# Spreading a norm over five units, ordering weight splits behind norm factors, and giving an operand rows of 512 floats

## The chip, the cores and the metric

The kernel runs on one core of a Trainium2 chip. The metric is device microseconds of an execution; the median of three executions of the kernel before is 1996.99 us (1993.12 to 1997.41). One further execution was profiled. PE is TensorE (matmul), PEld its weight loads, DVE is VectorE, ACT ScalarE, POOL GpSimd, SP SyncE; PE's clock is granted at one of two levels, 1.2 or 2.4 GHz.

## What is computed

Two transformer programs run one after the other on 256 tokens of width 1024. The first block has two layers: a mixer, a cross-attention to a memory of 256 tokens, and a SwiGLU (`silu(h @ w_gate) * (h @ w_up)) @ w_down`, hidden width 2816). The second block takes the first one's output as latents `h` and a second stream, Context `hc` (256 tokens), through two layers with adaptive modulation. Cut to what matters:

```
for l in range(2):
    mod, mod_c = silu(c) @ w_mod[l] + b_mod[l], silu(c_ctx) @ w_mod[l] + b_mod[l]
    ac = rms_norm(hc, norm1_g[l]) * (1 + csc1) + csh1      # Context's first norm
    a  = rms_norm(h,  norm1_g[l]) * (1 + sc1)  + sh1
    ... a @ w_in[l]: pooling, spatial gate, attention over h and Context's keys, gates
    h = h + g1 * mix
    h = h + g2 * square(relu(modulated_norm(h) @ w_ff1[l])) @ w_ff2[l]
    # Context has the same steps in layer 0; in layer 1 only its keys and values are used
return rms_norm(h, final_g)
```

All results are fp32. The kernel keeps that accuracy by splitting each operand into a high and a low part of a faster type (`hi`, and `lo = x - hi`) and by three matmuls for one.

## The kernel before, in words

**Splits.** Weights come in pieces of 128 x 1024 floats (512 KB) from memory, on SP's DMA queue. `pieces` (L210) loads one into a `raw` buffer (three of them) and splits it: ACT copies `hi` (L280), DVE subtracts `lo` (L281). There are four `hi` and four `lo` buffers, so that splits run up to four pieces ahead of PE. A block is one accumulation of PE: `s_block` (L230) has the weights stationary and streams the activation, `m_block` (L259) the other way round, each with three matmuls for every 128 rows (L226 to L228). `s_pair` (L240) streams `hi` and `lo` of the activation together as 512 columns (L247) and then `hi` with the weight's low part (L248); `pair_sum` (L252) adds the halves on ACT and DVE.

**Order.** The program's text is traced in order, and a planner orders each engine's queue from it: among what is ready the earlier traced goes first, with times that the planner works out beforehand. What is traced late can so be issued early, when nothing earlier is ready. An engine executes its queue strictly in that order. `tc.issue_after(x)` orders what is traced inside it behind `x` on `x`'s engine, without a wait for `x` to finish. PSUM has eight banks: three `mm`, two `sc`, two `pv`, one `fmm`.

**Operands.** `op` (L514) holds the current normalised activation, `hi` and `lo`, as `[128, 8 feature blocks, 2, 514]`: columns 0 to 255 are the latents, 256 to 511 Context, and the last two are used in layer 1 alone, when columns 256 to 513 hold the latents before normalisation (`raw`, L1186) with the two columns of the modulation's shift. Layer 1's first two feed-forward parts work on `raw` and scale the result by the row of norm factors afterwards (L1265), so that PE need not wait for the norm.

**A norm** is: squares on ACT (L318) summed on DVE (L335), token sums on PE (`token_sums`, L347, matmuls L354), an rsqrt chain of ten short DVE instructions (L363, L290 to L298), two transposes on PE that spread the factors over partitions (L371), an ACT copy of them (`rows`, L375), and for each of eight feature blocks a product on DVE (L921), the high part on ACT (L923) and the low part on DVE (L924) (`modulated`, L917).

**Where the norms stand.** Context's first norm is a hook in the second SwiGLU: `swiglu` (L792) runs eleven units, each `hidden` (gate and up blocks, an activation) and `down` (w_down blocks into four kept banks), and calls the hook `context` (L932) once, at unit 4: it finishes the modulation of layer 0 (`modulation_done`, whose weights come on POOL's DMA queue), loads Context, squares and sums it and normalises all eight feature blocks. In `layer` (L985) with two streams (layer 0) the order is: Context's block 2 of the first projection, `norm()` (final norm of the first block and layer 0's first norm in one, L1323), Context's block 3, `finish()` (latents' operand), the latents' blocks 0 and 1. Layer 0's feed-forward norm (L1217) comes after the `w_o` blocks of each stream in turn; its first four `w_ff1` pieces are traced after both (L1241). Layer 1's first norm of the latents (L1318) is traced between the last `w_ff2` blocks of the latents and those of Context; its first projection's pieces after all (L1003), and Context's norm (L1321) after the latents' two blocks.

**Branches.** `attnT`, `poolT` and `sguT` (L979 to L981) hold the three branches' results as separate `hi` and `lo` tiles; their last readers are the gate blocks, ahead of the `w_o` blocks at which `raw` is written.

The call of the hook and the operand, as they stand:

```
        for u in range(9):
            if hook is not None and u == 4:
                hook()
            down([hidden(u)], False)
        down([hidden(9), hidden(10)], True)
...
    op_all = pool.tile([128, KD, 2, 514], F32R, name="op")
    op = tuple(op_all[:, :, i, :] for i in range(2))
```

Of the kernel before, what the change touches and what calls it, by code (L numbers as in the profile page):

```python
# [106 lines left out]
def kernel(ctx: ExitStack, tc: tile.TileContext, A: dict, out: bass.AP):  # L107
# [101 lines left out]

    def pieces(name, group, then=None):  # L210

        res = []
        for off, k0, kt, n in OFFSETS[name][group]:
# [6 lines left out]
            split(hi, lo, raw)  # L220
# [38 lines left out]
    def m_block(ps, ws, act, t, k0=0, whole=None):  # L259
# [4 lines left out]
        for w in ws:  # L264
            for k in range(w.kt):
                a = w.k0 + k + k0
                mm3(ps, ah[:, a, sl], al[:, a, sl], w.hi[:, k, :], w.lo[:, k, :],
                    w is whole[0] and k == 0, w is whole[-1] and k == w.kt - 1)
# [78 lines left out]
    def token_sums(sums, tag="mm", ticks=3):  # L347
# [8 lines left out]
        tick(ticks, last)  # L356
        return ps
# [9 lines left out]
    def rows(cols, scales=(1.0,), tag="mm"):  # L367
# [146 lines left out]
    op_all = pool.tile([128, KD, 2, 514], F32R, name="op")  # L514
# [15 lines left out]
    mem = {}  # L530
# [261 lines left out]
    def swiglu(l, nrm, nxt, hook=None):  # L792
# [40 lines left out]
        for u in range(9):  # L833
            if hook is not None and u == 4:
                hook()
# [81 lines left out]
    def modulated(l, which, fb, s, g, row):  # L917

        a = s1("a")
        sh = modT[:, l, 24 * which + fb, s:s + 1]  # L920
        nc.vector.scalar_tensor_tensor(a, (xT, mem["n"])[s][:, fb, :], g[:, fb, s:s + 1], row, op0=OP.mult, op1=OP.mult)  # L921
        hi, lo = (x[:, fb, s * 256:s * 256 + 256] for x in op)
        nc.scalar.activation(hi, a, AF.Identity, bias=sh, scale=1.0)  # L923
        nc.vector.scalar_tensor_tensor(lo, a, sh, f(hi), op0=OP.add, op1=OP.subtract)  # L924

    def all_modulated(l, which, stream, acc, tag="mm"):
        (row,) = rows(rstd_cols([acc], tag), tag=tag)
        g = gains(l, which)
        for fb in range(KD):
            modulated(l, which, fb, stream, g, row)  # L930
# [48 lines left out]
    attnT = (pool.tile([128, 4, 512], F32R, name="ath"), pool.tile([128, 4, 512], F32R, name="atl"))  # L979
    poolT = (pool.tile([128, 2, 512], F32R, name="plh"), pool.tile([128, 2, 512], F32R, name="pll"))  # L980
# [504 lines left out]
```

## Time and profile before

| | |
|---|---|
| median of three executions | 1996.99 us (1993.12 to 1997.41) |
| the profiled execution, its own time | 1994.0 us |
| its span, first to last instruction | 1991.9 us |
| mean granted clock of PE | 0.991 |
| instructions | 32614, of them 12676 matmuls |

The span is what the trace's rows are measured in; 2.1 us of the execution lie around it. Busy time is time in which an engine has at least one instruction under way. PE's matmuls are pipelined and their ends are modelled, so a busy PE can still start matmuls at different spacings. A granted clock of 0.90 for a stretch means that a fifth of it ran at the lower level. Idle time is put down to what ended it.

### The profile page before, as it was taken

The numbers are of one execution on the slowest core, as the hardware profiler recorded it, in microseconds if no ns is written. First come the engines' busy times: TensorE is split into PE (matmuls) and PEld (weight loads), VectorE is DVE, ScalarE is ACT, GpSimd is POOL, SyncE is SP. The second block draws the span as 40 slices with busy tenths as digits, with TensorE's granted clock in tenths as the row PEclk, the third lists the DMA queues.
The fourth block names the chain that finished last, engine by engine and source line by source line (L and its number), as shares of the span: only waits on it lengthen the run. The fifth ranks groups of instructions, "written<-read, shape, count | busy, mean of one in ns | idle before, by whom it ended". The sixth has DMA issues, their size and how long they took to land.

```text
span 1991.9 us, 32614 instructions
## 1 busy us (share of the span) xinstructions
PE 1940.7 (97%) x12676; PEld 1701.0 (85%) x12676; DVE 1412.0 (71%) x2964; ACT 902.6 (45%) x1595; POOL 84.6 (4%) x163
## 2 busy tenths in 40 slices
PE   7999999999999899999999999999999999999998
PEld 6689999998988799698778888888888898899987
DVE  7677777777676777645677757777765855678897
ACT  5555555554554455424432234322223534555554
POOL 1100000000000000000011100110000000000000
PEclk9999999999999999999999999999999999999999
DMA  7746555553356555222245533444432422454553
GB/s 262 264 174 215 190 189 183 179 180 127 128 189 218 181 182 174 94 85 75 65 153 185 164 111 100 148 143 149 138 122 85 159 102 90 161 186 169 185 190 117
DMA packets 89771, 309.33 MB, mean 155 GB/s; under 512 B 10528, under 2 KB 15552, under 8 KB 89360
## 3 DMA queue, kind: packets, MB, share of 16 engines
q1 hardware_dynamic: 74048, 254.43, 37.3%
q0 software_dynamic: 15280, 52.28, 7.9%
q8 instruction: 100, 1.64, 0.3%
q14 instruction: 55, 0.45, 0.1%
q10 hardware_dynamic: 288, 0.52, 0.1%
HBM read 306.15 MB, written 1.05 MB: 154 GB/s over the span
## 4 chain that ended last, share of the span: by engine, by line
PE 92%; DVE 3%; issue 2%; ACT 1%; DMA 1%; POOL 0%; DVEq 0%; SPq 0%; POOLq 0%; ACTq 0%
PE mm L227 15%; PE mm L226 15%; PE mm L228 15%; PE mm L247 10%; PE mm L248 5%; PE sc L226 4%; PE sc L227 4%; PE sc L228 4%; PE pv L226 3%; PE pv L227 3%; PE pv L228 3%; PE sc L426 2%; PE pv L462 2%; PE pv L445 2%; DVE lo L281 1%
## 5 line engine op out<-in xcount | busy, mean ns | idle before, releaser
L280 ACT ACTIVATE hi<-raw 128x1024 fp32r<-128x1024 f32 (+2 forms) x466 | 489.6, 1054 | 714.8 <-PE mm L227 236.3
L281 DVE TENSOR_TENSOR lo<-raw,hi 128x1024 fp32r<-128x1024 f32 (+2 forms) x466 | 566.4, 1218 | 290.7 <-ACT hi L280 287.9
L226 PE MATMUL mm<-op,hi 128*128 128x256 f32 (+2 forms) x944 | 315.1, 336 | 3.9 <-ACT op L923 1.3
L227 PE MATMUL mm<-op,hi 128*128 128x256 f32 (+2 forms) x944 | 318.2, 338 | 0.0
L228 PE MATMUL mm<-op,lo 128*128 128x256 f32 (+2 forms) x944 | 318.0, 338 | 0.0
L247 PE MATMUL mm<-op,hi 128*128 128x512 f32 x872 | 310.8, 396 | 3.9 <-DVE g L256 3.6
L248 PE MATMUL mm<-op,lo 128*128 128x256 f32 x872 | 245.3, 281 | 0.0
L226 PE MATMUL mm<-hi,op 128*128 128x256 f32 (+2 forms) x704 | 210.3, 300 | 13.0 <-ACT hi L280 9.1
L227 PE MATMUL mm<-lo,op 128*128 128x256 f32 (+2 forms) x704 | 211.7, 301 | 1.3 <-DVE lo L281 1.3
L228 PE MATMUL mm<-hi,op 128*128 128x256 f32 (+2 forms) x704 | 209.7, 299 | 1.2 <-DVE op L284 1.2
L226 PEld LDWEIGHTS mm<-op,hi 128*128 128x128 f32 x944 | 178.7, 190 | 27.2 <-issue 3.4
L247 PEld LDWEIGHTS mm<-op,hi 128*128 128x128 f32 x872 | 165.3, 190 | 39.8 <-issue 4.3
L228 PEld LDWEIGHTS mm<-op,lo 128*128 128x128 f32 x944 | 178.8, 189 | 22.8 <-issue 2.9
L227 PEld LDWEIGHTS mm<-op,hi 128*128 128x128 f32 x944 | 178.9, 189 | 20.4 <-issue 1.4
L248 PEld LDWEIGHTS mm<-op,lo 128*128 128x128 f32 x872 | 165.1, 189 | 0.7 <-DVE gate L1172 0.4
L226 PEld LDWEIGHTS mm<-hi,op 128*128 128x128 f32 x704 | 136.0, 194 | 17.7 <-ACT hi L280 9.1
L227 PEld LDWEIGHTS mm<-lo,op 128*128 128x128 f32 x704 | 136.0, 193 | 9.8 <-issue 3.8
L228 PEld LDWEIGHTS mm<-hi,op 128*128 128x128 f32 x704 | 136.0, 193 | 8.3 <-issue 2.3
L161 POOL DMA_DIRECT2D mraw<-in_w_mod x96 | 51.5, 537 | 585.8 <-DVE modraw L163 579.6
L1192 DVE SCALAR_TENSOR_TENSOR xT<-pv,modT,xT 128x256 f32<-128x256 f32 x84 | 40.2, 481 | 43.1 <-PE pv L228 40.8
L163 DVE CUSTOM_DVE_ANT_0 fmm<-mraw,silu 128x512 f32<-128x512 f32 x96 | 66.7, 694 | 2.3 <-DMA mraw<-in_w_mod 2.3
L227 PE MATMUL sc<-hid,hi 128*128 128x512 f32 (+1 forms) x192 | 66.4, 346 | 1.6 <-DVE hid L1233 1.6
(349 smaller groups left out, 3822.8 us busy)
## 6 DMA issues: line engine op xcount, KB each, us to landing
raw<-in_w_ff SPq DMA_DIRECT2D x128, 512.0 KB, 3.3
raw<-in_w_in SPq DMA_DIRECT2D x84, 512.0 KB, 3.3
fraw<-in_w_mod POOLq DMA_DIRECT2D x48, 512.0 KB, 5.5
mraw<-in_w_mod POOLq DMA_DIRECT2D x96, 256.0 KB, 3.0
raw<-in_l_w_gate SPq DMA_DIRECT2D x44, 512.0 KB, 3.3
raw<-in_l_w_up SPq DMA_DIRECT2D x44, 512.0 KB, 3.3
raw<-in_l_w_down SPq DMA_DIRECT2D x44, 512.0 KB, 3.2
raw<-in_l_w_qkv SPq DMA_DIRECT2D x24, 512.0 KB, 3.5
```

Of the source, the lines that this page charges most:

```text
L161: nc.gpsimd.dma_start(out=w, in_=A["w_mod1"][c, i])
L163: nc.vector.tensor_tensor_reduce(out=w if s else bank("fmm"), in0=w, in1=silu[s][:, i * 512:i * 512 + 512], scale=1.0, scalar=0.0, op0=OP. ...
L226: nc.tensor.matmul(ps, ah, bh, start=start, stop=False, skip_group_check=shared)
L227: nc.tensor.matmul(ps, ah, bl, start=False, stop=False, skip_group_check=shared)
L228: return nc.tensor.matmul(ps, al, bh, start=False, stop=stop, skip_group_check=shared)
L247: nc.tensor.matmul(ps, w.hi[:, k, c0:c0 + 128], both[:, a], start=w is ws[0] and k == 0, stop=False)
L248: i = nc.tensor.matmul(ps[:, :256], w.lo[:, k, c0:c0 + 128], hi[:, a, :], start=False, stop=w is ws[-1] and k == w.kt - 1)
L280: nc.scalar.activation(hi, src, AF.Copy)
L281: nc.vector.tensor_sub(lo, src, f(hi))
L426: i = nc.tensor.matmul(ps, (ah, ah, al)[p], (bh, bl, bh)[p], start=p == 0, stop=p == 2)
L445: nc.tensor.transpose(ps[:, n:n + 128], P[t][:, c:c + 128], ident)
L1192: nc.vector.scalar_tensor_tensor(x, ps, gain, x, op0=OP.mult, op1=OP.add)
```

## The change

The hook is called at every unit: it loads Context and squares it at unit 3, finishes the modulation and works out the factors at unit 5 (in the `fmm` bank instead of an `mm` bank), and normalises three, three and two feature blocks at units 6, 7 and 8. In `modulated` each product on DVE is ordered behind the low part of the feature block two before. Splits of weights traced after a norm with `hold=True` are ordered on ACT behind the ACT copy of that norm's factors. Those norms are layer 0's first of the latents, layer 0's feed-forward norm of the latents, layer 1's first of the latents and layer 1's feed-forward norm. Pieces of the work that follows a norm are traced right after it, or before it in layer 1's feed-forward. At the start of layer 0, half of Context's block 3 is traced ahead of the norm and the other half ordered behind the norm's token sums; the latents' two blocks run piece by piece together (`early_blocks`, L617). In layer 1, Context's norm is ordered behind those blocks on PE. `op` has rows of 512 floats, the branches are one tile with `hi` and `lo` next to each other, and `raw` (now `unnormed`) lies in the same memory.

```diff
-    op_all = pool.tile([128, KD, 2, 514], F32R, name="op")
+    op_all = pool.tile([128, KD, 2, 512], F32R, name="op")
...
+    held = {}
     def pieces(name, group, then=None):
...
-            split(hi, lo, raw)
+            if "norm" in held:
+                with tc.issue_after(held["norm"].ins):
+                    split(hi, lo, raw)
+            else:
+                split(hi, lo, raw)
...
         tick(ticks, last)
+        held["sums"] = last
...
-            nc.scalar.activation(r, ps[:, :256], AF.Copy, scale=s)
+            i = nc.scalar.activation(r, ps[:, :256], AF.Copy, scale=s)
+            if hold:
+                held["norm"] = i
...
-                m_block(res[t][:, :n], [p], act, t, whole=w)
+                held["early"] = m_block(res[t][:, :n], [p], act, t, whole=w)
...
-            if hook is not None and u == 4:
-                hook()
+            if hook is not None:
+                hook(u)
...
+    def modulated(l, which, s, g, row, fbs=range(KD)):
+        lows = []
+        for fb in fbs:
...
+            if len(lows) > 1:
+                with tc.issue_after(lows[-2].ins):
+                    nc.vector.scalar_tensor_tensor(a, x, g[:, fb, s:s + 1], row, op0=OP.mult, op1=OP.mult)
...
+            lows.append(nc.vector.scalar_tensor_tensor(lo, a, sh, f(hi), op0=OP.add, op1=OP.subtract))
...
-    def context():
-        modulation_done(0)
-        mem["n"], acc = load_rows("ctx")
-        all_modulated(0, 0, 1, acc)
+    def context(u):
+        if u == 3:
+            mem["n"], mem["acc"] = load_rows("ctx")
+        elif u == 5:
+            modulation_done(0)
+            (mem["row"],) = rows(rstd_cols([mem["acc"]], "fmm"), tag="fmm")
+            mem["g"] = gains(0, 0)
+        elif u > 5:
+            modulated(0, 0, 1, mem["g"], mem["row"], range(3 * u - 18, min(3 * u - 15, KD)))
...
+    branches = pool.tile([128, 8 * 2 * 512], F32R, name="br")
+    parts = branches.rearrange("p (k a n) -> p a k n", k=8, a=2)
+    attnT, poolT, sguT = (tuple(parts[:, a, k:k + n, :] for a in range(2)) for k, n in ((0, 4), (4, 2), (6, 2)))
+    parts = branches[:, :KD * 2 * 272].rearrange("p (k a n) -> p k a n", k=KD, a=2)
+    unnormed = tuple(parts[:, a, :, 0:258] for a in range(2))
...
-            pooled_and_gated(2)
+            pg = pieces("w_in" + W, 6)
+            ps = mm()
+            m_block(ps, pg, op, 2)
+            pooled_and_gated(2, ps)
+            ps = mm()
+            m_block(ps, pg[:2], op, 3, whole=pg)
             finish, latents = norm()
-            pooled_and_gated(3)
+            with tc.issue_after(held["sums"].ins):
+                m_block(ps, pg[2:], op, 3, whole=pg)
+            pooled_and_gated(3, ps)
             finish()
...
+        for t, ps in enumerate(early_blocks(pg, op, 512)):
+            pooled_and_gated(t, ps)
+        if ns == 1:
+            with tc.issue_after(held["early"].ins):
+                norm()
...
-            raw = tuple(x[:, :, 256:514] for x in (op_all[:, :, 0, :], op_all[:, :, 1, :]))
+            raw = unnormed
...
-                all_modulated(l, 1, s, acc[s], "pv")
+                all_modulated(l, 1, s, acc[s], "pv", hold=s == 0)
+                if s == 0:
+                    first = [pieces("w_ff1" + W, j) for j in range(4)]
         else:
-            (row,) = rows(rstd_cols([acc[0]], "pv"), tag="pv")
+            first = [pieces("w_ff1" + W, j) for j in range(4)]
+            (row,) = rows(rstd_cols([acc[0]], "pv"), tag="pv", hold=True)
...
                 modulation_done(1)
-                all_modulated(l + 1, 0, 0, acc[0])
+                all_modulated(l + 1, 0, 0, acc[0], hold=True)
+                pg = pieces("w_in%d" % (l + 1), 6)
...
-            (row,) = rows(y[:, 2:4], tag="pv")
+            (row,) = rows(y[:, 2:4], tag="pv", hold=True)
```

## Rows read from the trace of the kernel before

**Rows 1.** The page, part 1: busy time, share of the span, instructions of each engine.

```profile
PE 1940.7 (97%) x12676; PEld 1701.0 (85%) x12676; DVE 1412.0 (71%) x2964; ACT 902.6 (45%) x1595; POOL 84.6 (4%) x163
```

**Rows 2.** Windows (us): length, busy time (instructions) by engine, granted clock, DMA share, GB/s.

```profile
655.00:690.00 35.00, 27.60 (x164) 25.08 (x163) 24.91 (x56) 16.26 (x29) 0.00 (x0) 0.90 0.43 143
...
700.00:760.00 60.00, 60.00 (x394) 54.84 (x393) 43.89 (x71) 30.44 (x50) 0.00 (x0) 1.00 0.54 184
...
793.50:833.00 39.50, 34.76 (x158) 25.60 (x157) 26.83 (x71) 19.05 (x38) 0.98 (x2) 0.91 0.32 107
...
1181.00:1206.00 25.00, 22.99 (x166) 22.59 (x166) 17.15 (x48) 9.78 (x18) 0.00 (x0) 0.86 0.25 85
...
1545.00:1575.00 30.00, 27.59 (x174) 23.77 (x172) 22.90 (x52) 16.13 (x28) 0.00 (x0) 0.94 0.44 158
...
1575.00:1600.00 25.00, 22.50 (x179) 21.59 (x176) 21.70 (x61) 10.04 (x20) 0.99 (x2) 0.93 0.44 148
...
1797.00:1829.00 32.00, 28.72 (x236) 28.16 (x235) 26.98 (x67) 18.70 (x34) 0.00 (x0) 1.00 0.46 161
```

**Rows 3.** Waits of PE: tile and line, releaser, us in total, times, longest.

```profile
PE sc L226 <- ACT qk L280: 5.1, 3, 3.8
...
PE mm L247 <- DVE g L256: 3.6, 1, 3.6
...
PE pv L354 <- DVE acc L335: 2.6, 2, 2.4
...
PE mm L226 <- DVE s L407: 2.4, 1, 2.4
```

**Rows 4.** Groups of DVE, 668 to 684: count, busy us, mean ns, idle before, releaser.

```profile
L281 DVE TENSOR_TENSOR lo<-raw,hi 128x1024 fp32r<-128x1024 f32 x5 | 6.1, 1224 | 4.6 <-ACT hi L280 4.6
...
L924 DVE SCALAR_TENSOR_TENSOR op<-a,modT,op 128x256 fp32r<-128x256 f32 x8 | 3.7, 480 | 0.0
...
L921 DVE SCALAR_TENSOR_TENSOR a<-memc,gain,rows 128x256 f32<-128x256 f32 x8 | 3.6, 479 | 0.0
```

**Rows 5.** Timeline, start of layer 0: start, us, instruction, idle before.

```profile
809.20 0.43 PE L371 MATMUL pv<-ident,sm 128*128 128x128 f32 x2 [2.63 <-DVE sm L298]
...
811.17 0.79 PE L226 MATMUL mm<-hi,op 128*128 128x512 f32 x1 [1.54 <-ACT op L923]
```

**Rows 6.** Windows of PE alone: `hid`, `op`; paired form on `hid`, on `op`.

```profile
1246.16:1267.92 21.76, 21.76 (x97) 1.00 0.45 147
...
1267.92:1290.30 22.38, 22.38 (x98) 1.00 0.43 142
...
1870.41:1874.57 4.16, 4.16 (x26) 1.00 0.49 182
...
720.53:726.13 5.60, 5.60 (x34) 1.00 0.48 164
```

**Rows 7.** Timeline of DVE and ACT, layer 0's feed-forward norm.

```profile
1184.81 0.16 DVE L363 TENSOR_SCALAR sm<-pv 128x2 f32<-128x2 f32 x1 [0.44 <-PE pv L354]
...
1188.40 1.23 DVE L281 TENSOR_TENSOR lo<-raw,hi 128x1024 fp32r<-128x1024 f32 x1
...
1189.55 0.15 DVE L298 SCALAR_TENSOR_TENSOR sm<-sm 128x2 f32<-128x2 f32 x1
...
1192.69 0.38 ACT L375 ACTIVATE rows<-pv 128x256 f32<-128x256 f32 x1 [1.13 <-PE pv L371]
```

**Rows 8.** Timeline of DVE and ACT, start of layer 1.

```profile
1554.35 0.15 DVE L298 SCALAR_TENSOR_TENSOR sm<-sm 128x2 f32<-128x2 f32 x1
...
1556.76 1.06 ACT L280 ACTIVATE hi<-raw 128x1024 fp32r<-128x1024 f32 x1 [1.14 <-PE pv L227]
...
1558.03 0.36 ACT L375 ACTIVATE rows<-mm 128x256 f32<-128x256 f32 x1
```

**Rows 9.** Groups of PE, shapes apart: paired form and one of three lines on `op`.

```profile
L247 PE MATMUL mm<-op,hi 128*128 128x512 f32 x872 | 310.8, 396 | 3.9 <-DVE g L256 3.6 <-ACT hi L280 0.3
...
L227 PE MATMUL mm<-op,hi 128*128 128x512 f32 x432 | 171.6, 397 | 0.0
```

More of the change, by code (lines that the diff above doesn't have):

```diff
@@ L266, in m_block @@
                 a = w.k0 + k + k0
-                mm3(ps, ah[:, a, sl], al[:, a, sl], w.hi[:, k, :], w.lo[:, k, :],
-                    w is whole[0] and k == 0, w is whole[-1] and k == w.kt - 1)
+                i = mm3(ps, ah[:, a, sl], al[:, a, sl], w.hi[:, k, :], w.lo[:, k, :],
+                        w is whole[0] and k == 0, w is whole[-1] and k == w.kt - 1)
+        return i
     def k_outer(jobs, act, n):
@@ L365, in rstd_cols, with rows @@
         return y
-    def rows(cols, scales=(1.0,), tag="mm"):
+    def rows(cols, scales=(1.0,), tag="mm", hold=False):
         ps = bank(tag)
@@ L915, in gains, with all_modulated @@
         return g
[L917 to L930, printed above, removed]
-    def context():
-        modulation_done(0)
-        mem["n"], acc = load_rows("ctx")
-        all_modulated(0, 0, 1, acc)
+    def modulated(l, which, s, g, row, fbs=range(KD)):
+        lows = []
+        for fb in fbs:
+            a = s1("a")
+            sh = modT[:, l, 24 * which + fb, s:s + 1]
+            x = (xT, mem["n"])[s][:, fb, :]
+            if len(lows) > 1:
+                with tc.issue_after(lows[-2].ins):
+                    nc.vector.scalar_tensor_tensor(a, x, g[:, fb, s:s + 1], row, op0=OP.mult, op1=OP.mult)
+            else:
+                nc.vector.scalar_tensor_tensor(a, x, g[:, fb, s:s + 1], row, op0=OP.mult, op1=OP.mult)
+            hi, lo = (x[:, fb, s * 256:s * 256 + 256] for x in op)
+            nc.scalar.activation(hi, a, AF.Identity, bias=sh, scale=1.0)
+            lows.append(nc.vector.scalar_tensor_tensor(lo, a, sh, f(hi), op0=OP.add, op1=OP.subtract))
+    def all_modulated(l, which, stream, acc, tag="mm", hold=False):
+        (row,) = rows(rstd_cols([acc], tag), tag=tag, hold=hold)
+        modulated(l, which, stream, gains(l, which), row)
+    def context(u):
[7 more added lines that the diff above has]
+            modulated(0, 0, 1, mem["g"], mem["row"], range(3 * u - 18, min(3 * u - 15, KD)))
     steps[0] = modulation_0()
@@ L1002, in layer, with pooled_and_gated @@
         mv = small.tile([128, 4, 2], F32, tag="mv", bufs=2, name="mv")
-        pg = pieces("w_in" + W, 6)
-        def pooled_and_gated(t):
-            ps = mm()
-            m_block(ps, pg, op, t)
+        def pooled_and_gated(t, ps):
             nc.scalar.activation(vt[:, t, :], ps[:, 256:], AF.Copy)
@@ L1240, in hidden @@
             if part == 0 and ns == 2:
-                ws = [pieces("w_ff1" + W, j) for j in range(4)]
                 for s in range(ns):
@@ L1244, in hidden @@
                         ps = mm()[:, :256]
-                        s_block(ps, ws[j], part_of(op, s))
+                        s_block(ps, first[j], part_of(op, s))
                         relu2(ps, hid, j, slice(s * 256, s * 256 + 256))
@@ L1252, in hidden @@
                     ps = mm() if j < 3 else bank("sc")
-                    w = pieces("w_ff1" + W, 4 * part + j)
+                    w = pieces("w_ff1" + W, 4 * part + j) if part else first[j]
                     if part == 0 and j < 3:
@@ L1300, in layer @@
             if part == 0 and ns == 1:
-                for fb in range(KD):
-                    modulated(l, 1, fb, 0, g2, row)
+                modulated(l, 1, 0, g2, row)
             second(part, *h)
@@ L1340, in finish @@
         def finish():
-            (row,) = rows(y[:, 2:4], tag="pv")
-            for fb in range(KD):
-                modulated(0, 0, fb, 0, gg, row)
+            (row,) = rows(y[:, 2:4], tag="pv", hold=True)
+            modulated(0, 0, 0, gg, row)
         def latents():
@@ L1350, in final_norm @@
         return finish, latents
-    context_norm = layer(0, 2, final_norm)
+    later = layer(0, 2, final_norm)
     fill.close()
-    acc = layer(1, 1, context_norm)
+    acc = layer(1, 1, later)
     ot = temp("memc", [128, 2, D])
```

12 lines of the change are left out of this document (3 added, 9 removed).

## The prediction, made before the changed kernel was run

> **What bounds the kernel now.** I began with the page's first part: PE is busy for 1940.7 of 1991.9 us, beside its weight loads no other engine over 71% [rows 1]. The reader should see that only 51 us of PE idleness exist, so the change can win from three things: idle stretches, matmuls that run on the lower clock after them, and the spacing of matmuls while PE is busy. I then cut the span into windows [rows 2]. The control stretch 700:760 has PE busy throughout at clock 1.00. The others hold the norms that the change touches; their idle time is the length less PE's busy time, and the granted clock tells what share ran at 1.2 instead of 2.4 GHz (0.90 is a fifth of the stretch at half speed, a tenth of its time lost):
>
> - 655:690, Context's norm in the swiglu: 7.4 idle, 3.5 lost to the clock
> - 793.5:833, start of layer 0: 4.7 and 3.5
> - 1181:1206, layer 0's feed-forward norm: 2.0 and 3.5
> - 1545:1575 and 1575:1600, start of layer 1: 2.4 and 1.8, 2.5 and 1.8
> - 1797:1829, layer 1's feed-forward: 3.3 and 0
>
> Together 36 us, the most that the ordering part can give. PE's waits [rows 3] say what ends the idleness: ACT and DVE, never a weight's landing directly. In each stretch the in-order queues of ACT and DVE hold weight splits beside the norm's short chain.
>
> **The change, step by step.** The profiled execution took 1994.0 us, 3.0 below the median 1996.99; I sum against 1994.0 and put 3.0 on at the end.
>
> **1. Context's norm spread over units.** Today hook 4 traces sixteen DVE instructions (eight L921, eight L924) of 0.48 us in one lump; between 668 and 684 they take 7.3 us of DVE beside five weight splits of 1.22 us, 6.1 [rows 4]. The pair sums and gating products that empty the `mm` banks come behind them, and PE waits 3.6 us for one of them (DVE g, L256) [rows 3]. After it, half of the window's clock loss follows, 1.7. Split into 3, 3 and 2 feature blocks, each later unit gets at most 6 x 0.48 = 2.9 us; in 700:760 DVE is idle for 60 - 43.9 = 16.1 us, over a quarter [rows 2], which hides that; the new order on DVE (each product behind the low part two blocks earlier) keeps them from bunching again. So 3.6 + 1.7 = 5.3 goes; I take 5.0. The window's other stall, PE waiting on ACT for `qk` (5.1 over three waits, the longest 3.8) [rows 3], is not in this lump. It belongs to splits held up while the last modulation weights and the next phase's loads go out, which the change re-traces but doesn't remove: 0. Bounds: 0 if the lump only moves, 7.4 + 3.5 = 10.9 if all goes. The ctx load (SP queue) and squares move from hook 4 to hook 3, 1 MB as before; no wait of PE names them [rows 3], so 0; the remaining modulation loads, on POOL, move from hook 4 to hook 5, and behind them on POOL stand only block 2's first loads, which need the modulation's memory. Moving sums and rows from `mm` to the `fmm` bank frees a bank that the swiglu uses; in the 5.0.
>
> **2. Start of layer 0.** After the token sums PE waits 2.63 for the rsqrt chain, turns the factors at 809.20, waits 1.54 for the first operand and starts at 811.17 [rows 5], then runs at the lower clock. The change leaves the second half of Context's block 3 for this hole: 2 pieces x 2 x 3 = 12 matmuls of 512 columns, at 22.38/96 = 0.233 us each [rows 6] 2.8 us. That covers the 2.63 wholly; the 1.54 stays. With idleness cut from 4.2 to about 1.6 I take the clock drop as avoided: 3.5 [rows 2]. `early_blocks` takes both token halves piece by piece, 6 matmuls or 1.4 us per feature block against 0.96 of DVE for its two instructions (2 x 0.48) [rows 4], so the operand is not late; but both halves then end together and their four ACT copies no longer hide behind the other half, about +1. 2.8 + 3.5 - 1 = 5.3; I take 5.0. Bounds: +1 (nothing covered, only the copies) to -8.2.
>
> **3. Layer 0's feed-forward norm.** The chain from L363 (1184.81) to L298 (1189.55) takes 4.7 us, with a 1.23 us split in it [rows 7]; at layer 0's start PE waits only 2.63 for a like chain [rows 5]. The factors are copied at 1192.69. Pinning the four splits behind that copy frees chain and copy, some 3 us; the price is that hi (1.06) [rows 8] and lo (1.23) [rows 7] of the first weight now come after it, on a DVE that has 16 x 0.48 to do as well. The pin is an order on ACT, no wait on another engine; behind a pinned split stand the norm's own ACT copies and stream 1's squares, each up to 1.06 later. Cover for this are stream 1's last `w_o` blocks on PE. I take 2.5 of the 5.5 there; bounds +3.7 (three splits of 1.23 that no longer lie ahead of the norm) and -5.5.
>
> **4. Start of layer 1.** The same shape: the chain ends at 1554.35, but a 1.06 split (1556.76) stands before the copy at 1558.03 [rows 8], and PE also waits 2.4 for stream 1's sums (DVE acc) [rows 3], which now queue behind the early blocks (behind them on PE only the factors' transposes; the keys of Context need those later). PE goes on instead with 48 matmuls of layer 1's first projection. Its four weight loads pass four small table loads on SP, nothing else. Nearly all of 2.4 + 1.8 should go: 4.0. The later stall (DVE s, 2.4 [rows 3]) comes from a DVE that stays as full: 0. Bounds +3.7 and -8.5.
>
> **5. Layer 1's feed-forward.** Hoisted first pieces and splits pinned behind the factors change the order on a DVE that is busy for 27.0 of 32 us [rows 2]; its sum is the same. 0; bounds +3.4 (a new clock drop like the others) and -3.3.
>
> **6. The operand without its two spare columns.** `op` shrinks from rows of 514 to 512 floats; the unnormalised operand goes to the branches' memory, whose readers finish before its first write, so no wait is added. What this may change is spacing. In 1267.92:1290.30 PE does four feed-forward blocks, 96 matmuls of 512 columns that stream `op`: 22.38 us, 233.1 ns each. Just before, the same form streams `hid` (rows of 512 floats): 96 in 21.76, 226.7 ns, both windows full and at clock 1.00 [rows 6] (the counts there include one or two still draining). The weights are laid out alike; the moving operand's place differs. Layer 0 has 3 x 432 such matmuls on `op` [rows 9]: 1296 x 6.4 ns = 8.4 us. The paired form costs 5.60/16 = 350 ns on `op` and 4.16/12 = 347 on `hid` [rows 6]: 872 pairs [rows 9] x 3 = 2.6. Of 11.0 I take 9.0, since each rate rests on one stretch. Bounds 0 to -11.
>
> Sentence apart: the Trainium skill (TensorE: Matmul & The Clock Gate, section Back-to-back issue gap) gives the spacing by the number of columns and the weight load, 518 cycles for 512 columns, with no term for where the operand lies; by it step 6 gives nothing and the sum is 16.5.
>
> **Sum:** 5.0 + 5.0 + 2.5 + 4.0 + 0 + 9.0 = 25.5. 1994.0 - 25.5 = 1968.5 for an execution like the profiled one, 1971.5 as a median; say **1971**.
>
> **Rivals.**
>
> *B, the spacing doesn't depend on the operand's place:* for it, that within a block the same operand is read by two neighbouring matmuls whose spacings differ; against it, that `hid` keeps one pace and `op` another in neighbouring windows. Then 1997 - 16.5 = 1980.
>
> *C, queue order doesn't follow trace order, or DVE's work decides:* the norms' instructions fill DVE wherever they go, and steps 1, 3 and 4 only move their stalls. For it, DVE's 27.0 of 32 and 21.7 of 25 us [rows 2]. Steps 2 and 6 stay: 1997 - 14 = 1983.
>
> *D, slower: the pinned split is the new last wait.* Place: the first matmul after each of the norms of steps 3, 4 and 5. Today three of four splits lie ahead of the norm; pinned, 3 x 1.23 = 3.7 us come behind the factors on DVE, and a longer hole adds a clock loss like the 3.5 seen: 7.1 at three sites, +21. It decides where PE reaches the first pinned weight before its lo is written. With steps 1 and 2 as above (-10) and B true: 2008. With step 6 working: 1999, no change that can be told.
>
> *E, the change does little at all* (the order comes out as before and the spacing too): 1997.
>
> **How the numbers follow.** A measurement of this kernel tells about 0.2%, 4 us, from no change. My forecast has 0.55, B 0.14, C 0.15, D with B 0.07, D with step 6 or E 0.09. Faster: 0.55 + 0.14 + 0.15 = 0.84; same 0.09; slower 0.07. The range: 1958 is the forecast with step 1's and step 4's whole ceilings (5.9 + 4.5 more, and 3 of step 3); 1990 takes in B and C with half of step 2 missing. The forecast alone would span 1960 to 1982.
>
> **What would show it.** Step 1: in the unit that now ends near 684, PE without the wait on DVE g and no clock drop after it. Step 2: PE's wait for L298 gone, clock 1.00 over the early blocks. Steps 3 and 4: no `hi` split between sums and factor copy, PE idle under 1 us. Step 6: `op` blocks at 21.8 us per 96. Wrong: first waits on `lo` after a norm (D), or `op` at 233 ns still (B).

## The result and the profile after

The changed kernel takes 1972.4 us (median of four executions, 1971.6 to 1974.46) against 1997.12 for the kernel before: ratio 0.9882, 95% interval 0.9865 to 0.99. The forecast was 1971. The profiled execution took 1973.03 us with a span of 1970.9. The total came out nearly as forecast; its terms did not. (For an execution like the profiled one the forecast was 1968.5, against 1973.03: the median fits better because the profiled execution of the kernel before lay 3 us below its median, and that of the changed kernel does not.)

The page's first part, as in [rows 1]:

```profile
PE 1929.8 (98%) x12676; PEld 1695.9 (86%) x12676; DVE 1411.6 (72%) x2964; ACT 902.6 (46%) x1595; POOL 84.8 (4%) x163
```

Of the 21.0 us by which the span shrank, 10.9 are PE time that was busy before (1940.7) and 10.1 idle time. The windows of [rows 2], moved so that each begins and ends with the same matmul by count (the length, then busy time of PE, PEld, DVE, ACT and POOL, then PE's clock):

```profile
656.36:681.16 24.80, 24.66 (x163) 22.46 (x162) 18.72 (x40) 12.84 (x21) 0.00 (x0) 1.00 0.62 207
691.08:751.45 60.37, 60.37 (x394) 54.95 (x393) 49.55 (x88) 33.73 (x58) 0.00 (x0) 1.00 0.53 184
785.17:818.85 33.68, 31.24 (x158) 23.68 (x156) 25.80 (x69) 18.08 (x37) 0.09 (x1) 0.95 0.36 125
1166.36:1188.40 22.04, 20.41 (x167) 19.81 (x166) 16.62 (x44) 9.70 (x17) 0.00 (x0) 1.00 0.29 96
1523.88:1552.43 28.55, 25.80 (x173) 22.80 (x172) 23.45 (x55) 15.73 (x27) 0.00 (x0) 1.00 0.38 133
1552.43:1575.32 22.89, 21.22 (x179) 20.17 (x176) 21.29 (x58) 10.34 (x19) 1.02 (x2) 1.00 0.43 151
1773.30:1806.07 32.77, 29.92 (x236) 28.93 (x235) 26.67 (x65) 18.18 (x33) 0.00 (x0) 0.97 0.44 156
```

Context's norm: 35 us became 24.80, both stalls and the low clock are gone. Layer 0's start: idle 4.7 became 2.4 (33.68 - 31.24), and the clock still falls (0.95). At layer 0's feed-forward norm and at layer 1's start PE is idle nearly as long as before (2.0 became 1.6; 2.4 + 2.5 became 2.75 + 1.67), but the clock stays at 1.00. Layer 1's feed-forward got longer. PE's waits, as in [rows 3] (the first is the start of the program):

```profile
PE mm L233 <- ACT hi L288: 9.0, 1, 9.0
PE mm L233 <- ACT op L941: 3.7, 3, 1.9
PE mm L254 <- ACT hi L288: 2.8, 2, 2.5
...
PE mm L234 <- DVE op L942: 1.1, 1, 1.1
PE mm L235 <- DVE op L942: 1.1, 1, 1.1
```

The waits for `qk` (3.8), `g` (3.6), the rsqrt chain (2.6) and `acc` (2.4) are gone; first operands and one weight of layer 1's feed-forward stand in their place.

**A table for all runs.** Every kernel issues 12,676 matmuls, so each trace gives the time at which PE begins the n-th. Below is the time that each stretch takes in each profiled execution, less that of the kernel before. The stretches begin in the kernel before at: start 0; A 164.8 (first block); B 636.7 (Context's norm); C 707.4 (to layer 0's start); D 844.5; E 1179.4 (layer 0's feed-forward norm); F 1221.6 (layer 0's feed-forward); G 1537.3 (layer 1's start); H 1598.8; I 1767.5 (layer 1's feed-forward, first parts); J 1878.1 to 1984.0.

```
kernel                start     A     B     C     D     E     F     G     H     I     J     A-J
the change              0.6   0.7 -10.1  -3.0  -2.8  -2.2  -4.3  -3.6   0.9   1.7   0.8  -21.9
E1 rows 512 alone      -0.6   0.6   0.9  -1.0  -2.8  -1.3  -4.3  -0.5   1.3   0.3   0.8   -6.0
E2 op 8 bytes on        3.5   2.6  -7.0  -1.6   0.4  -2.3   0.4  -1.9   0.9   2.3   0.8   -5.5
E11 rest 32 bytes on    6.1  -0.7 -10.2  -2.5  -0.0  -1.0   0.3  -1.9  -0.1   0.5   0.2  -15.5
E3 hook in mm           3.3   0.6  -8.3  -4.7  -2.8  -2.2  -4.3  -3.6   0.9   1.7   0.8  -21.9
E4 lump in fmm         -0.7   0.7  -8.0  -5.2  -2.8  -2.2  -4.3  -3.6   0.9   1.7   0.8  -22.1
E8 no half block        0.6   0.6 -10.2  -0.1  -2.8  -2.9  -4.3  -2.2   0.9   1.7   0.8  -18.4
E5 no pins              6.8   0.7 -10.5  -4.7  -2.8  -2.8  -4.3  -1.6   0.9   1.7   0.8  -22.5
E6 pin behind op       -0.3   0.7 -10.4  -3.0  -2.8  -2.6  -4.3  -2.4   0.9   1.6   0.8  -21.4
E7 no ff1 pin           2.0   2.1 -10.5  -4.6  -2.8  -2.2  -4.3  -3.6   0.9   1.7   0.8  -22.4
E9 no order             0.3   0.7  -9.9  -4.5  -2.8  -2.2  -4.3  -0.9   0.9   2.6   0.8  -19.6
E10 neither             1.2   0.7 -10.1  -3.0  -2.8  -1.3  -4.3   0.1   1.1   0.3   0.8  -18.5
E12 pin once            2.5   2.2 -10.2  -4.7  -2.8  -1.3  -4.3  -1.9   0.9   1.8   0.8  -19.5
```

Two things are to be seen. D, F and J repeat to 0.1 us in all kernels that share their code there. The start does not: it varies by 7 us between the profiled executions, though in all fourteen traces the instructions come in the same order up to A; E3 reaches A 2.7 us later than the changed kernel. There is one trace of each kernel, so whether one kernel's own executions differ as much there is not shown. I therefore don't rank kernels by medians that differ by less than about 5 us, but by the stretches, with the caution on the clock that comes below.

### The profile page after: what moved, and what is told of

Read it like the earlier page. It is cut to its first block, busy times and chain, and to the rows that moved or that the text cites. A ratio compares the mean times of both kernels' runs of the same rounds, so it can differ in the third digit from the quotient of the medians.

```text
span 1970.9 us, 32609 instructions
## 1 busy us (share of the span) xinstructions
PE 1929.8 (98%) x12676; PEld 1695.9 (86%) x12676; DVE 1411.6 (72%) x2964; ACT 902.6 (46%) x1595; POOL 84.8 (4%) x163
## 4 chain that ended last, share of the span: by engine, by line
PE 93%; DVE 3%; DMA 1%; issue 1%; ACT 1%; POOL 0%; DVEq 0%; SPq 0%; POOLq 0%; ACTq 0%
PE mm L233 15%; PE mm L234 15%; PE mm L235 15%; PE mm L254 10%; PE mm L255 5%; PE sc L233 4%; PE sc L234 4%; PE sc L235 4%; PE pv L233 3%; PE pv L234 3%; PE pv L235 3%; PE sc L437 2%; PE pv L473 2%; PE pv L456 2%; PE fmm L140 1%; DVE lo L289 1%
## 5 line engine op out<-in xcount | busy, mean ns | idle before, releaser
L234 PE MATMUL mm<-op,hi 128*128 128x256 f32 (+1 forms) x896 | 300.2, 336 | 1.1 <-DVE op L942 1.1
L235 PE MATMUL mm<-op,lo 128*128 128x256 f32 (+1 forms) x896 | 300.4, 337 | 0.0
L233 PE MATMUL mm<-op,hi 128*128 128x256 f32 (+1 forms) x896 | 297.9, 337 | 2.1 <-ACT relu L1261 1.1
L254 PEld LDWEIGHTS mm<-op,hi 128*128 128x128 f32 x872 | 163.9, 188 | 39.2 <-ACT hi L288 3.3
L235 PEld LDWEIGHTS mm<-op,lo 128*128 128x128 f32 x896 | 169.7, 189 | 21.2 <-issue 2.9
L233 PEld LDWEIGHTS mm<-op,hi 128*128 128x128 f32 x896 | 167.8, 189 | 22.7 <-issue 2.0
L234 PEld LDWEIGHTS mm<-op,hi 128*128 128x128 f32 x896 | 169.7, 189 | 20.1 <-issue 1.7
L255 PEld LDWEIGHTS mm<-op,lo 128*128 128x128 f32 x872 | 164.8, 189 | 1.0 <-DVE gate L1201 0.4
L163 DVE CUSTOM_DVE_ANT_0 mraw<-mraw,silu 128x512 f32<-128x512 f32 x96 | 66.1, 688 | 2.1
```

The costliest lines, as they stand in the source:

```text
L163: nc.vector.tensor_tensor_reduce(out=w if s else bank("fmm"), in0=w, in1=silu[s][:, i * 512:i * 512 + 512], scale=1.0, scalar=0.0, op0=OP. ...
L233: nc.tensor.matmul(ps, ah, bh, start=start, stop=False, skip_group_check=shared)
L234: nc.tensor.matmul(ps, ah, bl, start=False, stop=False, skip_group_check=shared)
L235: return nc.tensor.matmul(ps, al, bh, start=False, stop=stop, skip_group_check=shared)
L254: nc.tensor.matmul(ps, w.hi[:, k, c0:c0 + 128], both[:, a], start=w is ws[0] and k == 0, stop=False)
L255: i = nc.tensor.matmul(ps[:, :256], w.lo[:, k, c0:c0 + 128], hi[:, a, :], start=False, stop=w is ws[-1] and k == w.kt - 1)
```

## The experiments

### E1: the rows of 512 floats alone

On the kernel before: `op` in rows of 512, the branches in one tile, the unnormalised operand in it.

```diff
-    op_all = pool.tile([128, KD, 2, 514], F32R, name="op")
+    op_all = pool.tile([128, KD, 2, 512], F32R, name="op")
...
-            raw = tuple(x[:, :, 256:514] for x in (op_all[:, :, 0, :], op_all[:, :, 1, :]))
+            raw = unnormed
```

> The kernel before with step 6 alone (op in rows of 512 floats, the unnormalised operand in the branches' memory, nothing of the order changed). If the spacing depends on the operand's place, the four feed-forward blocks on op take 21.8 us instead of 22.4 (226.7 ns for each of 96 matmuls), 1296 of them give 8.4, and the whole comes to 1989, 0.4% faster than before. Rival B (no effect of the place): 233.1 ns stay and the whole stays at 1997. All the waits of before, the 3.8 for qk and the 3.6 for g among them, stay under both.

1988.85 us, ratio 0.9969 (0.9957 to 0.998), A to J 6.0 us less. The two windows of [rows 6], PE alone, on `hid` and then on `op`:

```profile
1241.43:1263.19 21.76, 21.76 (x97) 1.00 0.43 145
1263.19:1284.95 21.76, 21.76 (x97) 1.00 0.45 146
```

96 matmuls on `op` now take as long as on `hid`: rival B falls. In F 672 such matmuls give 4.3 us, the forecast 6.4 ns each. But A, B and H to J cost 3.9 (0.6 + 0.9 + 1.3 + 0.3 + 0.8).

Not all of this is spacing. E1's windows of Context's norm and of layer 0's feed-forward norm:

```profile
655.16:690.82 35.66, 28.70 (x163) 25.85 (x162) 24.79 (x56) 16.31 (x29) 0.00 (x0) 0.86 0.42 144
...
1178.08:1201.81 23.73, 21.74 (x168) 21.31 (x166) 17.19 (x48) 9.82 (x18) 0.00 (x0) 0.93 0.26 89
```

E1 has the order of the kernel before there and nearly its idle time (6.96 against 7.40, 1.99 against 2.01 [rows 2]), but the clock is 0.86 against 0.90, and 0.93 against 0.86. So the +0.9 in B and the -1.3 in E are mostly the clock. C's -1.0 also comes at the same idle time (5.36 in both); PE is busy at the lower level there for 3.9 us instead of 5.9. Stretches in which the clock stays up in both traces (A, D, F, I, J) give 5.4.

Nor is the paired form the main cost. A block of 288 matmuls of 256 columns with `op` stationary, in D, PE alone, in the kernel before, in E1 and in E11 (below):

```profile
845.55:879.77 34.22, 34.22 (x291) 1.00 0.23 78
```

```profile
845.43:880.07 34.64, 34.64 (x291) 1.00 0.23 78
```

```profile
838.32:872.33 34.01, 34.01 (x291) 1.00 0.26 78
```

So this form too got slower with the rows of 512, by 1.5 ns each. An estimate from the starts of all matmuls in both traces: 256-column matmuls on `op` cost about 2.5 us, pairs about 1.6. The prediction priced only the pairs.

### E2: the rows start 8 bytes later

```diff
-    op_all = pool.tile([128, KD, 2, 512], F32R, name="op")
+    op_flat = pool.tile([128, KD * 2 * 512 + 2], F32R, name="op")
+    op_all = op_flat[:, 2:].rearrange("p (k a n) -> p k a n", k=KD, a=2)
```

> The changed kernel with op's rows still 512 floats apart, but all of them starting 2 floats (8 bytes) later. If what costs is where a row starts, the spacing on op goes back up from 226.7 to 231 to 236 ns, 1296 matmuls cost 6 to 12 us, and the whole comes to 1978 to 1984. If what costs is the distance of the rows (514 against 512 floats), the spacing stays at 226.7 and the whole at 1972.

1990.21 us, ratio 0.9973 (0.9962 to 0.9983): slower than either answer expected. The window on `op`, PE alone:

```profile
1263.48:1285.89 22.41, 22.41 (x98) 1.00 0.44 140
```

22.41 for 96 is the kernel before again, with rows 512 apart: the distance of the rows is not it. That it is where a row starts was the obvious reading, and E11 shows it to be wrong; this edit also moved all that lies behind `op`, by 32 bytes (so the addresses in the built kernels say). What E2 loses beyond E11 was not taken apart; part of it is the paired form on `op`, 40 pairs of which take 14.31 us in A, against 14.12 in E11 and 13.87 in the changed kernel.

### E11: `op` where it was, all behind it 32 bytes on

```diff
-    op_all = pool.tile([128, KD, 2, 512], F32R, name="op")
+    op_flat = pool.tile([128, KD * 2 * 512 + 8], F32R, name="op")
+    op_all = op_flat[:, :KD * 2 * 512].rearrange("p (k a n) -> p k a n", k=KD, a=2)
```

> The changed kernel with op where it is, its rows of 512 floats, and all that lies behind it in memory (weights, hidden values, branches) 32 bytes further on, by 8 unused floats at op's end. If only op's own row starts count, the 512-column matmuls on op stay at 226.7 ns and the whole at 1972. If the distance between the streamed operand and the weights counts, they rise to 229 to 233 and the whole to 1975 to 1980. The paired form on hid, 352.8 ns in the changed kernel and 348.1 with the same 32 bytes in the shifted run, comes back to 348 if the place of what lies behind op decides it: 1 us less.

1979.82 us, ratio 0.9919 (0.9903 to 0.9934). The windows on `hid` and on `op`, PE alone:

```profile
1237.88:1259.66 21.78, 21.78 (x97) 1.00 0.45 147
1259.66:1282.07 22.41, 22.41 (x98) 1.00 0.45 141
```

`op` has not moved and its matmuls are slow again; `hid` and the weights moved together, and that pair is as fast as ever. So what counts is how the streamed operand and the weights lie to each other in memory, not the place of either. Removing the two spare columns of `op`'s 16 rows (32 floats, 128 bytes) changed both: the rows' starts and the distance to the weights. The paired form on `hid`, PE alone, the last 32 pairs of layer 1, first in the kernel before, then changed, then in E11:

```profile
1958.62:1969.61 10.99, 10.99 (x66) 1.00 0.42 146
```

```profile
1937.14:1948.33 11.19, 11.19 (x65) 1.00 0.41 144
```

```profile
1949.24:1960.23 10.99, 10.99 (x66) 1.00 0.46 146
```

6 ns a pair went with the change and came back with 32 bytes, though `hid` and its weights kept their distance. This is the sign of step 6's other half; its cause stays open.

### E3 and E4: the hook's bank and its lump, one at a time

```diff
-            (mem["row"],) = rows(rstd_cols([mem["acc"]], "fmm"), tag="fmm")
+            (mem["row"],) = rows(rstd_cols([mem["acc"]], "mm"), tag="mm")
```

> The changed kernel, but Context's token sums and factors use an mm bank again instead of fmm; the spread over units stays. Theory from the two traces: the bank is what removed PE's 3.8 us wait for qk (with the sums in a third mm bank PE could not begin the next gate block and stood before the down blocks), so that wait and about 1.7 us of half clock come back: 1976 to 1978. Rival (the spread alone did all of the gain of about 10 us at the hook): 1972, no wait for qk over 1 us.

```diff
             mem["g"] = gains(0, 0)
-        elif u > 5:
-            modulated(0, 0, 1, mem["g"], mem["row"], range(3 * u - 18, min(3 * u - 15, KD)))
+            modulated(0, 0, 1, mem["g"], mem["row"])
```

> The changed kernel, but all eight feature blocks of Context's norm at unit 5 in one lump; sums and factors stay in the fmm bank. The prediction's step 1: the sixteen instructions of 0.48 us in a lump hold up the product that empties an mm bank, the wait for g of 3.6 us and 1.7 us of half clock come back: 1977 to 1978. Rival (the bank did it all, the lump is harmless once PE has a free mm bank): 1972 to 1973, no wait for g over 1 us.

E3 1977.36 (0.9909, 0.9895 to 0.9922), E4 1972.62 (0.9891, 0.9875 to 0.9906). PE's waits between 640 and 720, E3, then E4:

```profile
PE sc L233 <- ACT qk L288: 1.8, 1, 1.8
```

```profile
PE mm L254 <- DVE a L263: 0.8, 1, 0.8
PE mm L255 <- DVE lo L289: 0.5, 1, 0.5
```

Spread, but in the `mm` bank, B gains 8.3: a wait of 1.8 for `qk` comes back, without a fall of the clock. In a lump, but in the free bank, it gains 8.0. Both together 10.1. Either edit suffices for most of it; neither theory had it alone. Both kernels share a third part, the load and squares at unit 3 instead of 4, but it isn't what frees the first stall. In the kernel before and in E4 the token sums begin at the same time (657.8), and up to there PE, DVE and ACT have the same order. Then, with the sums in an `mm` bank, PE comes to blocks that read `qk` and stands; with the bank free it has a block of the paired form to do until `qk` is there. PE in the kernel before, E4, and E3 (bank `mm` again, later sums):

```profile
658.65 0.36 PE L354 MATMUL mm<-ones,sq 128*128 128x1 f32 x2
662.84 0.50 PE L226 MATMUL sc<-qk,hi 128*128 128x256 f32 x2 [3.83 <-ACT qk L280]
```

```profile
658.84 0.36 PE L362 MATMUL fmm<-ones,sq 128*128 128x1 f32 x2
659.19 0.39 PE L255 MATMUL mm<-op,lo 128*128 128x256 f32 x1
```

```profile
679.68 0.36 PE L362 MATMUL mm<-ones,sq 128*128 128x1 f32 x2
681.81 0.39 PE L233 MATMUL sc<-qk,hi 128*128 128x256 f32 x1 [1.77 <-ACT qk L288]
```

The second stall, for `g`, is less clear: in E4 the lump also comes a unit later (factors copied at 677.4 instead of 669.8), and that alone was not run. The order of the products, which E3 and E4 share too, isn't needed (E9 and E10 below: B -9.9 and -10.1). E3's median is 5 us up with A to J equal to the changed kernel's: 2.7 of it is the start in the profiled execution, the rest I can't place.

### E8: block 3 whole ahead of the norm

```diff
-            m_block(ps, pg[:2], op, 3, whole=pg)
+            m_block(ps, pg, op, 3)
             finish, latents = norm()
-            with tc.issue_after(held["sums"].ins):
-                m_block(ps, pg[2:], op, 3, whole=pg)
```

> The changed kernel with Context's block 3 whole ahead of the norm again, instead of one half of it behind the token sums. Step 2: the half block (12 matmuls, 2.9 us) covers the rsqrt chain; without it PE waits 2.6 us for it again and the low clock lasts longer: 1975 to 1977. Rival (the half block only moves the wait to the operand): 1972 to 1973.

1976.68 (0.9908, 0.9895 to 0.9922). The wait that comes back, and the windows of layer 0's start and of layer 1's start:

```profile
PE pv L380 <- DVE sm L306: 2.6, 1, 2.6
```

```profile
785.00:821.61 36.61, 32.10 (x157) 24.32 (x156) 25.55 (x69) 18.39 (x37) 0.09 (x1) 0.91 0.36 115
...
1525.89:1555.79 29.90, 27.16 (x173) 23.82 (x172) 23.60 (x55) 15.85 (x28) 0.00 (x0) 0.94 0.39 134
```

As the theory had it: the half block is worth 2.9 us in C. The second row is the caution: layer 1's start has the changed kernel's code, its order on PE (on DVE and ACT a few instructions have changed places) and the same idle time (29.90 - 27.16 = 2.74 against 2.75), and yet the clock falls here (0.94) and G gains 2.2 instead of 3.6. E11 has the changed kernel's order on all engines throughout; its windows of layer 0's feed-forward norm, layer 1's start and layer 1's feed-forward:

```profile
1173.68:1197.01 23.33, 21.70 (x167) 21.10 (x166) 17.41 (x48) 9.69 (x17) 0.00 (x0) 0.93 0.27 91
1537.02:1567.37 30.35, 27.59 (x173) 23.96 (x172) 23.65 (x55) 15.84 (x28) 0.00 (x0) 0.94 0.39 132
...
1787.06:1819.10 32.04, 29.00 (x235) 28.20 (x234) 26.09 (x64) 18.20 (x34) 0.00 (x0) 1.00 0.46 150
```

PE is idle for 1.63, 2.76 and 3.04 us (changed kernel: 1.63, 2.75 and 2.85). The clock falls at the first two, where it stayed up in the changed kernel, and stays up at the third, where it fell.

### E5, E9 and E10: no pins, no order of the products, neither

```diff
-                held["norm"] = i
+                pass
```

> The changed kernel without any pin: splits of weights are no longer ordered behind the norms' factors, everything else stays. Theory (steps 3 and 4): a hi split stands again between the token sums and the factors' copy at layer 0's feed-forward norm and at layer 1's start, PE waits longer there and the clock falls again: the 2.2 and 3.4 us that the two traces show at these places go in large part, 1975 to 1978. Rival D (the pinned splits are the new last wait, since three of them in a row now stand on ACT between the factors' copy and the first operand, and PE loses 1.9 and 3.2 us there): without pins it is as fast or faster, 1969 to 1972.

```diff
-            if len(lows) > 1:
+            if False:
```

> The changed kernel without the order of the products on DVE (each behind the low part two blocks before); pins and all else stay. Theory, from the run without pins (which kept the gain of layer 0's feed-forward norm with the same late factors as the kernel before): this order is what earns step 3, since without it four products and a split come ahead of the first low part; then PE waits 1 to 2 us longer for low parts there and the clock may fall: 1974 to 1977. Rival (the pins and the order each suffice): 1972, the stretch unchanged. A third possibility: the order costs in layer 1's feed-forward, where the change loses 2 us; then these come back there.

E10 has both edits.

> The changed kernel without pins and without the order of the products: what is left is the bank, the half block, the blocks piece by piece, the pieces traced earlier and the rows of 512. If the product order earns step 3, its gain goes as in the run with pins (1974 to 1977); if pins or order suffice alone, only here does the stretch come out like the kernel before, with some 3 us lost at layer 0's feed-forward norm and 2 at layer 1's start: 1976 to 1979.

E5 1971.63 (0.9888, 0.9873 to 0.9904), E9 1976.91 (0.9912, 0.9894 to 0.9931), E10 1977.64 (0.9903, 0.9886 to 0.992). Layer 0's feed-forward norm on the timeline, first E5, then the changed kernel:

```profile
1173.38 1.06 ACT L288 ACTIVATE hi<-raw 128x1024 fp32r<-128x1024 f32 x1 [2.05 <-PE mm L234]
...
1179.17 0.15 DVE L306 SCALAR_TENSOR_TENSOR sm<-sm 128x2 f32<-128x2 f32 x1
...
1182.31 0.39 ACT L384 ACTIVATE rows<-pv 128x256 f32<-128x256 f32 x1 [1.13 <-PE pv L380]
...
1184.41 0.62 PE L233 MATMUL mm<-op,hi 128*128 128x256 f32 x3 [1.31 <-ACT op L941]
```

```profile
1175.36 0.38 ACT L384 ACTIVATE rows<-pv 128x256 f32<-128x256 f32 x1 [1.28 <-PE pv L380]
1175.64 2.94 ACT L288 ACTIVATE hi<-raw 128x1024 fp32r<-128x1024 f32 x3
...
1178.48 0.90 ACT L941 ACTIVATE op<-a,modT 128x256 fp32r<-128x256 f32 x2
...
1181.30 0.39 PE L234 MATMUL mm<-op,hi 128*128 128x256 f32 x1 [1.14 <-DVE op L942]
```

Without pins the splits lie in the chain as in [rows 7] and the factors come as late; E still gains 2.8, where the changed kernel gains 2.2. With pins the factors come early, and three splits in a row then stand on ACT between them and the operand. The pins moved the wait by one instruction. Windows of layer 0's feed-forward norm and the first of layer 1's start, E5, E9 and E10:

```profile
1170.56:1192.00 21.44, 20.04 (x167) 19.75 (x166) 16.99 (x48) 10.02 (x17) 0.00 (x0) 1.00 0.31 99
1527.49:1557.96 30.47, 27.13 (x173) 23.99 (x172) 24.05 (x55) 16.50 (x28) 0.00 (x0) 0.94 0.49 170
```

```profile
1164.78:1187.60 22.82, 20.40 (x167) 19.80 (x166) 17.20 (x46) 9.47 (x17) 0.00 (x0) 1.00 0.30 93
1522.33:1553.31 30.98, 27.43 (x174) 23.94 (x172) 24.04 (x55) 15.75 (x28) 0.00 (x0) 0.94 0.37 118
```

```profile
1166.89:1190.62 23.73, 21.74 (x167) 21.31 (x166) 17.20 (x48) 9.92 (x18) 0.00 (x0) 0.93 0.28 89
1525.35:1555.97 30.62, 27.28 (x173) 23.92 (x172) 23.87 (x55) 16.18 (x28) 0.00 (x0) 0.94 0.49 171
```

PE's idle time at layer 0's feed-forward norm is 1.4 (order alone), 2.4 (pins alone), 2.0 (neither), 1.6 (both): the order saves 0.6 to 0.8, the pins nothing. At layer 1's start it is 3.3, 3.55, 3.3 and 2.75: there the two save 0.6 together, and nothing singly. The other differences in E and G are mostly the clock's. E9's third possibility falls: I loses 2.6 without the order, more than with it.

### E6, E7 and E12: attempts at something better

E6 pins behind the second ACT copy of the operand instead of the factors' copy (in `modulated`, at feature block 1).

> The changed kernel with the splits pinned behind the second high part of the operand (the ACT copy of feature block 1) instead of behind the factors' copy. Theory: the three splits of 1.05 us that ACT now does between factors and operand are what PE waits for (1.9 us at layer 0's feed-forward norm, 3.2 at layer 1's start); with the operand first, PE gains about 1 us at each place: 1970 to 1971. Rival: the first weight's low part is then the last to come, and nothing is gained or 1 to 2 us are lost: 1972 to 1974.

E7 leaves `hold=True` out of layer 1's feed-forward norm.

> The changed kernel without the pin in layer 1's feed-forward alone. In the two traces the change loses 2.1 us there: the wait of 1.5 at the norm went, but PE stands 2.5 us later for a weight's high part and then runs 3.4 us at the lower clock. If the pin causes that (it lets the raw buffers go later, so that the following loads leave late), the loss goes and the whole comes to 1970. Rival (DVE is full there, whatever the order): the time stays within 1 us of 1972, the wait only sits in another place.

E12 keeps `hold=True` at layer 1's first norm alone and leaves the products of layer 1's feed-forward without order.

> The changed kernel with what the runs so far speak for: splits pinned only behind layer 1's first norm (the one place where leaving the pin out cost more than 1 us, 1.9), products on DVE ordered everywhere but in layer 1's feed-forward (where the run without pins and without that order is 1.3 to 1.4 us faster than the runs with either). Theory: 0.6 us less at layer 0's feed-forward norm, 1.4 less in layer 1's feed-forward, 0 to 1.6 less at layer 0's start, where the clock falls in some kernels and not in others: 1969 to 1971, the fastest of all. Rival (each stall only moves to the next place): 1972 and over.

E6 1977.86 (0.99, 0.9885 to 0.9914), E7 1972.12 (0.988, 0.9867 to 0.9893), E12 1973.65 (0.989, 0.9875 to 0.9905): none beats the changed kernel by what can be told. E6's rival holds: PE waits up to 2.2 us for low parts of weights instead. E7's and E12's theories fall: the loss of 1.7 in I stays in both; only E10 and E11 are rid of most of it, and both keep the clock at 1.00 there. E7's window of layer 0's start:

```profile
787.56:819.66 32.10, 29.66 (x158) 22.55 (x156) 25.80 (x69) 18.09 (x37) 0.09 (x1) 1.00 0.41 131
```

Up to layer 1's feed-forward E7 has the changed kernel's instructions in the same order on PE, DVE and ACT. PE is idle as long here (32.10 - 29.66 = 2.44, as 33.68 - 31.24), the clock does not fall, and C gains 4.6 instead of 3.0. E12's windows of layer 0's feed-forward norm and of layer 1's feed-forward:

```profile
1168.02:1190.95 22.93, 21.54 (x167) 21.25 (x166) 17.00 (x48) 10.03 (x17) 0.00 (x0) 0.93 0.29 93
...
1777.53:1809.90 32.37, 29.24 (x235) 28.68 (x234) 27.65 (x69) 19.41 (x36) 0.00 (x0) 0.98 0.49 162
```

The first is the same thing the other way round: E5's order of instructions, E5's idle time (1.39 against 1.40), and the clock falls here where it did not there. E gains 1.3 instead of 2.8.

## Why the prediction was right, and where it was not

A to J give 21.9 us where the steps summed to 25.5. The prices below are read against E1, which has step 6 alone. So they carry the difference between E1's falls of the clock and those of the kernel before, up to 1.5 us in B, C and E each; what they become against the kernel before stands at the end.

**Step 1: 5.0 forecast, 10.9 measured** (B: -10.1 against +0.9; 10.1 against the kernel before): nearly the whole ceiling of 10.9, or all of it. The step that failed is the sentence that the stall for `qk` "belongs to splits held up while the last modulation weights and the next phase's loads go out, which the change re-traces but doesn't remove: 0". Those loads are still there, the stall is not. With the bank, to which I gave no price of its own, or with the spreading most of both stalls is gone (E4, E3), and the wait for `qk` belonged to the bank that the sums held.

**Step 2: 5.0 forecast, 2.0 measured** (C: -3.0 against -1.0). The half block covers the rsqrt wait as worked out. The copies' cost of 1 is not shown: E8's C is 0.9 worse than E1's, but in PE's busy time (131.75 against 130.67), not in idle time (5.18 against 5.36). What failed is "I take the clock drop as avoided: 3.5": half of it is still there (0.95). In E7, with the same instructions and the same idle time, the clock stays and C gains 1.6 more: cutting the idleness did not rule the fall out.

**Step 3: 2.5 forecast, 0.9 measured** (E: -2.2 against -1.3, both with the clock's uncertainty). The mechanism failed: "Pinning the four splits behind that copy frees chain and copy, some 3 us". It does free them, and the splits then hold the operand back (timeline above). I had priced only their low parts on DVE and the norm's copies behind a pinned split "up to 1.06 later"; it was three in a row. That part of rival D is real; it cancels the pins' gain instead of outweighing it. The order of the products, which I mentioned under step 1 alone, is what shortens the idle time here.

**Step 4: 4.0 forecast, 3.1 measured** (G: -3.6 against -0.5), but not as argued: the waits named are gone and others came, idle time falls by 0.5 only (the sign "PE idle under 1 us" failed here as in step 3), and the rest is a clock that happened to stay up. In E8 and E11 it did not, and G gave 1.7 and 1.4.

**Step 5: 0 forecast, a loss of 1.4** (I: +1.7 against +0.3), within the bounds. The waits of before (1.6 for `hid`, 1.2 and 0.5 for `scaled`) went; PE then stands 2.5 for a weight's high part, and the clock falls (0.97), though PE is idle for less than before (2.85 against 3.3, then in several pieces, at 1.00). Which edit does it is open: without pins and order the loss is gone (E10), but leaving both out in that layer keeps it (E12), and E11, which changes nothing of the order, has only 0.5 of it, with PE idle for longer (3.04) and the clock at 1.00.

**Step 6: 9.0 forecast, 6.0 measured** (E1), rival B refuted. The size of the first term was right. Two others were not: the paired form was to give part of 2.6 and cost some 1.6, and the 256-column matmuls on `op`, which the sum leaves out, cost some 2.5 (estimates, E1). By the Trainium skill (TensorE: Matmul & The Clock Gate, section Back-to-back issue gap) the step gives nothing; 21.76 against 22.38 for the same 96 matmuls disagrees, and the measurement decides. And the reason was incomplete: the step worked because 514 to 512 also moved `op` and the weights into a better distance. With 8 more floats behind `op` the same step would have lost most of its gain (E11).

So the total was right by luck: step 1 was 5.9 too low and the others 9.9 too high (3.0 + 1.6 + 0.9 + 1.4 + 3.0); the other stretches give 0.4. Against the kernel before, steps 1 to 5 read 10.1, 3.0, 2.2, 3.6 and -1.7 (B, C, E, G, I), and step 6 reads 4.7 from A, D, F, H and J, where it alone acts: the same 21.9, with step 6 off by more than 4. Rival C is near the truth for the idle time of steps 3 and 4. And the prediction's prices of the clock (3.5 each for the first three norms) count idle time in as lost: PE was busy at the lower level for 6.3, 5.9 and 6.4 us there, which loses 3.1, 2.9 and 3.2.

## What to carry to other kernels

Before costing an in-order jam by the instructions in it, list every resource that the lump holds, PSUM banks too: here two ways out of the same jam did not add up (8.0 and 8.3 singly, 10.1 together). A split that is pinned out of one chain stands ahead of whatever comes next on its queue: count how many are ready at that moment. And where a matmul's spacing matters, compare blocks that stream different tiles in the same trace; a few floats of padding between operand and weights were worth 6 ns in 227 on every matmul of one form here, and the other way on another form, so measure the padding as a parameter, and over all forms.

## What the runs showed of the hardware

The spacing of full 512-column matmuls goes from 226.7 to 233 ns with the distance in memory between the streamed operand and the weights (21.76 against 22.41 us for 96; 32 bytes suffice, E11). Other forms have several paces as well, by a rule that I did not find: the paired form on `hid` 10.99 or 11.19 us for the same 32 pairs, 288 matmuls of 256 columns with `op` stationary 34.22, 34.64 or 34.01 us. 32 bytes bring both from the changed kernel's slow pace to a faster one (E11), while they cost the 512-column form 6 ns.

PE's clock does not follow from the instructions and the idle time alone: with the same order and idle times equal to 0.01 us it fell at layer 0's start in the changed kernel and not in E7, at layer 0's feed-forward norm in E12 and not in E5, at layer 1's start in E11 (whose matmuls differ in spacing) and not in the changed kernel. Each fall costs 1.4 to 1.6 us. A site's gain read from one execution each is uncertain by that much.

The first 165 us vary by 7 us between the profiled executions of these kernels, with the same order of instructions. With differences of a few microseconds between kernels, the stretches after it tell more than the medians.
